# Log-sum-exp over rows: the first load from one contiguous block, its results stored early

## Chip, cores, metric

One core of one Trainium2 chip. The metric is the device time of one execution in microseconds (us); unless said otherwise a time is a median over runs of one kernel. All runs here were single-core, at a granted clock of 1.0. A profiled span is about 1.8 us shorter than the time of the same execution.

Loads are numbered as in the code, from 0 to 16. The prediction's "fifth load" is load 4.

## The reference

```python
# x: (32, 512, 1024) float32, drawn from N(0, 1); axis = -1
def reference(x, axis):
    x_max = np.max(x, axis=axis, keepdims=True)
    return (x_max.squeeze(axis) + np.log(np.sum(np.exp(x - x_max), axis=axis))).astype(np.float32)
```

There are 16384 rows of 1024 values (67.1 MB), and one result for each row. For this draw all results lie between 7.28 and 7.60. So the comparison with the reference cannot see results that are merely in the wrong place.

## The kernel before

Each of the 128 partitions owns 128 consecutive rows. They come in 17 loads of 1 to 16 rows a partition, all on SyncE's DMA queue, into a ring of 51 rows. ScalarE does Exp on each load. For the first `n_dve` rows of a load VectorE adds up the exponentials; for the others ScalarE adds them up itself, row by row. Two Ln instructions on ScalarE turn sums into results, and one store writes 64 KB at the end.

```python
CHUNKS = [   # rows a partition, rows summed by VectorE
    (4, 1), (15, 11), (16, 10), (16, 15), (16, 0), (14, 0), (12, 9), (9, 5), (7, 5), (5, 4),
    (4, 3), (3, 0), (2, 2), (2, 2), (1, 0), (1, 0), (1, 0),
]
RING_ROWS = 51
LN_AT = 5                     # the first Ln comes before load 5's work
...
    x_v = x_flat.rearrange("(p t) d -> p t d", p=P)                       # 512 KB from partition to partition
    out_v = bass.AP(tensor=out.tensor, offset=out.offset, ap=[[NB, P], [1, NB]])
...
    def load(i):              # waits until its ring rows are free, then
        ... nc.sync.dma_start(out=ring[:, s : s + r], in_=x_v[:, row : row + r]).then_inc(landed[i], 16)
...
    for i, (r, n_dve) in enumerate(CHUNKS):
        if i:
            load(i)
        if i == LN_AT:
            take_logs(0, logged, *done_before[i])
        nc.scalar.wait_ge(landed[i], 16)
        ... Exp, and the sums ...
    take_logs(logged, NB, dves, acts)
    nc.scalar.wait_ge(act_done, acts)
    nc.scalar.dma_start(out=out_v, in_=res).then_inc(stored, 16)
    nc.gpsimd.wait_ge(stored, 16)
```

The softmax here doesn't subtract the row's maximum and nothing guards it: scores larger than these inputs give would overflow.

## Time and profile before

| | before |
|---|---|
| time, 3 runs | 164.23 us (164.02 to 164.56) |
| span of the profiled run | 162.2 us |
| ScalarE busy | 124.1 us, 76% |
| load 0 / load 4 / load 5 has landed | 7.40 / 83.67 / 100.65 us |
| last wait of ScalarE for a load ends | 83.69 us |
| last store, issue to landing | 1.57 us |

The landing times and the store's 1.57 us are from the trace's records of semaphore updates, which have two digits; the page rounds them. A load has landed when the last of its 16 DMA queues has reported to its semaphore; on each queue it consists of eight packets. From the page of the kernel before (engines' busy time; DMA queues with packets, MB and the share of 16 DMA engines; issues with size and us to landing):

```profile
span 162.2 us, 213 instructions
DVE 72.9 (45%) x11; ACT 124.1 (76%) x136; POOL 0.2 (0%) x4
...
q1 hardware_dynamic: 2448, 67.11, 96.4%
q10 hardware_dynamic: 144, 0.07, 0.1%
q14 instruction: 1, 0.01, 0.0%
HBM read 67.11 MB, written 0.07 MB: 414 GB/s over the span
...
out_dram<-res ACTq DMA_DIRECT2D x1, 64.0 KB, 1.6
```

q1 carries all loads and is busy for 96.4% of the span, so DMA is the first limit. q14 is a fetch of instructions that the program does not ask for. The timeline of ScalarE (start, duration, line, operation; in brackets the idle time before it and what ended it) shows every wait for a load:

```profile
7.42 1.06 ACT L116 ACTIVATE ring<-ring 128x1024 f32<-128x1024 f32 x1 [5.37 <-DMA ring<-in_x_dram]
25.62 9.59 ACT L116 ACTIVATE ring<-ring 128x11264 f32<-128x11264 f32 x1 [14.02 <-DMA ring<-in_x_dram]
44.98 8.74 ACT L116 ACTIVATE ring<-ring 128x10240 f32<-128x10240 f32 x1 [5.62 <-DMA ring<-in_x_dram]
64.36 13.00 ACT L116 ACTIVATE ring<-ring 128x15360 f32<-128x15360 f32 x1 [4.42 <-DMA ring<-in_x_dram]
83.69 1.06 ACT L128 ACTIVATE ring<-ring 128x1024 f32<-128x1024 f32 x1 [5.29 <-DMA ring<-in_x_dram]
```

After 83.69 us ScalarE is busy without a break until the last store. But it is a close race: load 10 landed at 145.61 us and was used at 145.65, load 11 landed at 149.30 and was used at 149.34. Any delay of the stream over 0.04 us shows. Some pieces of the chain of waits (start, us, what), which has no load after 83.67 us:

```profile
47.15 36.52 DMA ring<-in_x_dram
83.67 0.02 issue
83.69 10.55 ACT ring L128 x21
...
148.40 4.16 ACT ring L128 x8
...
159.36 0.25 ACT res L93
```

Windows of the kernel before (stretch, its length, busy time of VectorE, ScalarE and GpSimd with the number of instructions, clock, DMA share, GB/s; a packet is counted whole where it starts, so short windows swing):

```profile
60.00:84.00 24.00, 11.17 (x2) 14.35 (x4) 0.00 (x0) 1.00 1.00 431
...
146.00:148.00 2.00, 2.00 (x1) 2.00 (x1) 0.00 (x0) 1.00 1.00 424
148.00:150.00 2.00, 2.00 (x2) 2.00 (x4) 0.00 (x0) 1.00 0.97 406
```

### The profile page before, as it was taken

The numbers are of one execution on the slowest core, as the hardware profiler recorded it, in microseconds if no ns is written. First come the engines' busy times: TensorE is split into PE (matmuls) and PEld (weight loads), VectorE is DVE, ScalarE is ACT, GpSimd is POOL, SyncE is SP. The second block draws the span as 40 slices with busy tenths as digits, with TensorE's granted clock in tenths as the row PEclk, the third lists the DMA queues.
The fourth block names the chain that finished last, engine by engine and source line by source line (L and its number), as shares of the span: only waits on it lengthen the run. The fifth ranks groups of instructions, "written<-read, shape, count | busy, mean of one in ns | idle before, by whom it ended". The sixth has DMA issues, their size and how long they took to land.

```text
span 162.2 us, 213 instructions
## 1 busy us (share of the span) xinstructions
DVE 72.9 (45%) x11; ACT 124.1 (76%) x136; POOL 0.2 (0%) x4
## 2 busy tenths in 40 slices
DVE  0030000039960799000999900000006999799591
ACT  3180006997099971999339999999999999999993
POOL 0000000000000000000000000000000000000000
DMA  6999899969969959969988999999999999999970
GB/s 263 497 485 470 349 394 517 485 291 517 485 291 517 517 259 517 517 275 501 517 368 370 424 424 432 461 497 388 436 427 399 431 400 439 420 424 414 415 318 16
DMA packets 2593, 67.18 MB, mean 414 GB/s; under 512 B 288, under 2 KB 416, under 8 KB 800
## 3 DMA queue, kind: packets, MB, share of 16 engines
q1 hardware_dynamic: 2448, 67.11, 96.4%
q10 hardware_dynamic: 144, 0.07, 0.1%
q14 instruction: 1, 0.01, 0.0%
HBM read 67.11 MB, written 0.07 MB: 414 GB/s over the span
## 4 chain that ended last, share of the span: by engine, by line
ACT 52%; DMA 38%; DVE 7%; issue 1%
DMA ring<-in_x_dram 38%; ACT ring L128 30%; ACT ring L116 22%; DVE sums L121 7%; ACT res L93 0%
## 5 line engine op out<-in xcount | busy, mean ns | idle before, releaser
L121 DVE TENSOR_REDUCE sums<-ring 128x5 f32<-128x5120 f32 (+8 forms) x11 | 72.9, 6648 | 86.0 <-ACT ring L116 85.9
L116 ACT ACTIVATE ring<-ring 128x5120 f32<-128x5120 f32 (+8 forms) x11 | 59.3, 5394 | 29.4 <-DMA ring<-in_x_dram 29.4
L128 ACT ACTIVATE ring<-ring 128x1024 f32<-128x1024 f32 x61 | 63.4, 1041 | 5.3 <-DMA ring<-in_x_dram 5.3
L128 ACT ACTIVATION_READ_ACCUMULATOR ring<-ring 128x1 f32 x61 | 11.4, 187 | 0.0
L103 ACT ACT_TABLE_LOAD x1 | 1.3, 1283 | 0.8 <-PEq L175 0.8
L93 ACT ACTIVATE res<-sums 128x67 f32<-128x67 f32 (+1 forms) x2 | 0.5, 256 | 0.1
L175 POOL MEMSET const-bfloat16-1.0<- 128x1 bf16 x1 | 0.1, 101 | 0.0
L175 POOL MEMSET const-uint8-127<- 128x1 uint8 x1 | 0.1, 101 | 0.0
L175 POOL MEMSET const-float32-0.0<- 128x1 f32 x1 | 0.1, 98 | 0.2 <-issue 0.2
L175 POOL MEMSET const-float32-1.0<- 128x1 f32 x1 | 0.1, 98 | 0.0
## 6 DMA issues: line engine op xcount, KB each, us to landing
ring<-in_x_dram SPq DMA_DIRECT2D x1, 7680.0 KB, 24.8
ring<-in_x_dram SPq DMA_DIRECT2D x1, 7168.0 KB, 36.1
ring<-in_x_dram SPq DMA_DIRECT2D x1, 6144.0 KB, 21.6
ring<-in_x_dram SPq DMA_DIRECT2D x1, 4608.0 KB, 32.1
ring<-in_x_dram SPq DMA_DIRECT2D x2, 2048.0 KB, 26.3
ring<-in_x_dram SPq DMA_DIRECT2D x1, 3584.0 KB, 40.2
ring<-in_x_dram SPq DMA_DIRECT2D x1, 2560.0 KB, 44.4
ring<-in_x_dram SPq DMA_DIRECT2D x2, 1024.0 KB, 46.0
```

What stands on the lines that cost most here:

```text
L93: nc.scalar.activation(out=res[:, lo:hi], in_=sums[:, lo:hi], func=Ln).then_inc(act_done, 1)
L103: nc.scalar.preload_act_table_set("natural_log_exp_and_others")
L116: nc.scalar.activation(out=ring[:, s : s + n_dve], in_=ring[:, s : s + n_dve], func=Exp).then_inc(act_done, 1)
L121: nc.vector.reduce_sum(out=sums[:, row : row + n_dve], in_=ring[:, s : s + n_dve], axis=AX).then_inc(dve_done, 1)
L128: nc.scalar.activation(out=ring[:, s + j], in_=ring[:, s + j], func=Exp, accum_out=sums[:, row + j : row + j + 1],).then_inc(act_done, 1)
L175: nc = _bacc.Bacc("TRN2", target_bir_lowering=False, num_devices=1)
```

## The change

The intent: the first load no longer picks 16 KB out of each 512 KB of the input but reads one contiguous 2 MB. Each partition's other 124 rows follow in the rest of the input, with 496 KB from partition to partition (the pitch). The results of the first four rows now belong elsewhere in the output than the other 124. So there are two stores: 128 pieces of 16 bytes, issued between loads 10 and 11 on the queue of the loads, and 128 pieces of 496 bytes at the end. Both are packed: the next partition's piece begins where this one's ends.

```diff
-FIRST_PARTS = [("sync", 0, 128)]
+STORE_AT = 11
...
-    x_v = x_flat.rearrange("(p t) d -> p t d", p=P)
-    out_v = bass.AP(tensor=out.tensor, offset=out.offset, ap=[[NB, P], [1, NB]])
+    R0 = CHUNKS[0][0]
+    x_first = x_flat[: P * R0].rearrange("(p t) d -> p t d", p=P)
+    x_rest = x_flat[P * R0 :].rearrange("(p t) d -> p t d", p=P)
+    out_first = bass.AP(tensor=out.tensor, offset=out.offset, ap=[[R0, P], [1, R0]])
+    out_rest = bass.AP(
+        tensor=out.tensor, offset=out.offset + P * R0, ap=[[NB - R0, P], [1, NB - R0]]
+    )
+
+    def rows_of(row, r):
+        return x_first if row == 0 else x_rest[:, row - R0 : row - R0 + r]
...
+        nc.sync.dma_start(out=ring[:, s : s + r], in_=rows_of(row, r)).then_inc(landed[i], 16)
...
+        if i == STORE_AT:
+            nc.sync.wait_ge(act_done, logs_done)
+            nc.sync.dma_start(out=out_first, in_=res[:, :R0]).then_inc(stored_first, 16)
         if i:
             load(i)
...
-    nc.scalar.dma_start(out=out_v, in_=res).then_inc(stored, 16)
+    nc.scalar.dma_start(out=out_rest, in_=res[:, R0:]).then_inc(stored, 16)
+    nc.gpsimd.wait_ge(stored_first, 16)
     nc.gpsimd.wait_ge(stored, 16)
```

More of the change, by code (lines that the diff above doesn't have):

```diff
@@ L54 @@
     dve_done = tc.alloc_semaphore("dve_done")
+    stored_first = tc.alloc_semaphore("stored_first")
     stored = tc.alloc_semaphore("stored")
@@ L83, in load @@
             nc.sync.wait_ge(act_done, act_wait)
-        for engine, lo, hi in FIRST_PARTS if i == 0 else [("sync", 0, P)]:
-            getattr(nc, engine).dma_start(
-                out=ring[lo:hi, s : s + r], in_=x_v[lo:hi, row : row + r]
-            ).then_inc(landed[i], 16)
+        nc.sync.dma_start(out=ring[:, s : s + r], in_=rows_of(row, r)).then_inc(landed[i], 16)
     def take_logs(lo, hi, dve_wait, act_wait):
@@ L113 @@
             take_logs(0, logged, *done_before[i])
-        nc.scalar.wait_ge(landed[i], 16 * (len(FIRST_PARTS) if i == 0 else 1))
+            logs_done = acts
+        nc.scalar.wait_ge(landed[i], 16)
         if n_dve:
```

## The prediction

> **What bounds the kernel now.** The DMA stream first, with ScalarE tuned to finish just behind it. The page gives 67.11 MB read at 414 GB/s; the windows view gives 431 GB/s from 60 to 84 us and 430 from 84 to 100 us. In the trace's packet records every engine's queue runs without gaps from about 1.1 to 157.6 us, and steady packets take 2.42 us for 65536 B, 2.27 us for 61440 B, 0.61 us for 16384 B: each is 27 GB/s per engine, 433 GB/s for 16. So steady packets already run at one common rate, whatever the address. ScalarE is busy 124.1 us (76%). In the chain of waits the fifth load lands at 83.67 us; from then ScalarE never waits again and ends at 159.6. The chunk landings in that tail are early by very little (chunks 10 and 11 by 0.04 us, the last by 0.11 us): DMA and ScalarE are level. Then the store: issue at 159.64, landing 1.6 us later.
>
> **What the change does.** Bytes read, chunk sizes and the order on ScalarE and VectorE stay. The row pitch between partitions goes from 512 KB to 496 KB, the first load becomes one contiguous 2 MB, SyncE gets one extra store (128 pieces of 16 B), the last store's pieces go from 512 to 496 B.
>
> 1. Start. The first packet of each engine is slow: by 0.00 to 0.75 us over the later 0.61 us, about 0.3 us in the mean; second packets are nearly clean. If this is the 512 KB pitch, up to 0.3 us are won, and the whole chain moves with it. If it is plain first latency, nothing is won. I count 0.15 us.
> 2. Pitch. The Trainium skill, "DMA: Bandwidth & Descriptors", section "Latency and other measured facts", warns of power-of-two HBM row pitches: 207 GB/s per direction at 512 KiB against 214 padded, for HBM-to-HBM copies. This trace shows no such loss after the first packets (under 0.2 us in all from 10 to 120 us): 0.0.
> 3. Early store. It sits between loads 10 and 11 in the same queue. The 512 B packets of the present store take 27 ns each, so an estimate of 0.1 to 0.2 us of queue time, just where ScalarE has 0.04 us of slack. SyncE's wait for the logs (done 100.7 us) is free, as load 11 is held to 103.9 us. Cost: 0.1 us.
> 4. Last store. 496 B pieces that start at odd multiples of 16 B; the same page gives 512 B as the size below which a read-modify-write happens. The landing might grow from 1.6 to 1.7 us: 0.05.
>
> All four are critical, and nearly cancel.
>
> **Predicted:** 164.1 us (range 163.5 to 164.7); faster by over 2%: 0.01, within 2%: 0.98, slower by over 2%: 0.01.
>
> **What would show it.** First-load landing at 7.1 to 7.4 us (before 7.40); fifth load within 0.4 us of 83.67; the windows view still 430 GB/s from 60 to 100 us; waits of ScalarE on loads 11 to 16 of 0 to 0.2 us; last store landing at 1.6 to 1.8 us; ScalarE still 124.1 us busy.
>
> **What would make it wrong.** The contiguous block could [...]slow the first load; the 16-byte writes could hold their queue by more than a microsecond, which the tail would feel in full; or unprofiled runs may suffer more from the start than the profiled one, so that the gain is larger than 0.3 us.

## The result, and the profile after

| | before | after |
|---|---|---|
| time, 6 runs each | 164.43 us (164.02 to 164.56) | 164.93 us (164.64 to 165.27) |
| ratio | | 1.0036, 95% interval 1.0019 to 1.0054 |
| profiled span | 162.2 us | 163.2 us |
| load 0 / 4 / 5 landed | 7.40 / 83.67 / 100.65 us | 7.75 / 83.93 / 101.18 us |
| load 11 landed | 149.30 us | 150.02 us |
| last store, issue to landing | 1.57 us | 1.76 us |

Every ratio in this document is the mean time of one kernel's runs over the mean of the runs of before in the same rounds, so not quite the ratio of the medians. The change makes the kernel slightly slower. Run again beside other kernels it came to 1.0015 (1.0000 to 1.0029). So it costs a quarter to six tenths of a microsecond, and the prediction's range (up to 164.7 us) did not hold the first measurement. Part of that is the base: the three runs of before had a median of 164.23 us, the six of the comparison 164.43 us.

The page of the changed kernel:

```profile
span 163.2 us, 215 instructions
DVE 72.9 (45%) x11; ACT 124.2 (76%) x136; POOL 0.2 (0%) x4
...
q1 hardware_dynamic: 2592, 67.11, 96.3%
q10 hardware_dynamic: 144, 0.06, 0.1%
q14 instruction: 1, 0.01, 0.0%
HBM read 67.11 MB, written 0.07 MB: 412 GB/s over the span
...
out_dram<-res ACTq DMA_DIRECT2D x1, 62.0 KB, 1.8
...
out_dram<-res SPq DMA_DIRECT2D x1, 2.0 KB, 45.4
```

The work of the engines is the same. q1 has 144 more packets, the early store: 128 pieces and 16 semaphore packets. It waits 45.4 us in the queue, which costs nothing as such. The waits for loads that the timeline of ScalarE marks, after:

```profile
7.77 1.06 ACT L128 ACTIVATE ring<-ring 128x1024 f32<-128x1024 f32 x1 [5.71 <-DMA ring<-in_x_dram]
25.88 9.59 ACT L128 ACTIVATE ring<-ring 128x11264 f32<-128x11264 f32 x1 [13.94 <-DMA ring<-in_x_dram]
45.25 8.74 ACT L128 ACTIVATE ring<-ring 128x10240 f32<-128x10240 f32 x1 [5.62 <-DMA ring<-in_x_dram]
64.61 13.00 ACT L128 ACTIVATE ring<-ring 128x15360 f32<-128x15360 f32 x1 [4.39 <-DMA ring<-in_x_dram]
83.95 1.06 ACT L140 ACTIVATE ring<-ring 128x1024 f32<-128x1024 f32 x1 [5.31 <-DMA ring<-in_x_dram]
101.20 1.06 ACT L140 ACTIVATE ring<-ring 128x1024 f32<-128x1024 f32 x1 [0.22 <-DMA ring<-in_x_dram]
```

Load 0 comes 0.35 us later, not earlier, and there is a new wait for load 5. The chain of waits now goes through loads 5 and 11 (the wait for load 11, 0.16 us, is not marked above):

```profile
64.87 36.31 DMA ring<-in_x_dram
101.18 0.02 issue
101.20 3.23 ACT ring L140 x6
104.44 0.02 issue
104.45 45.57 DMA ring<-in_x_dram
150.02 0.02 issue
150.05 3.23 ACT ring L140 x6
...
160.08 0.25 ACT res L101
```

And the windows show where the stream slowed, just behind the early store (its packets run at 144.5 to 145.7 us):

```profile
60.00:84.00 24.00, 11.20 (x2) 14.31 (x6) 0.00 (x0) 1.00 1.00 431
...
146.00:148.00 2.00, 2.00 (x1) 2.00 (x3) 0.00 (x0) 1.00 1.19 412
148.00:150.00 2.00, 2.00 (x2) 1.98 (x3) 0.00 (x0) 1.00 0.77 303
```

The added span of this pair of profiles, from the trace records, is 0.99 us:

- 0.53 us: load 5 lands later (0.26 us are there at load 4 already; 0.27 us come between loads 4 and 5);
- 0.19 us: from load 5's landing to the issue of the last store (58.99 us before, 59.18 us after), nearly all of it the wait for load 11;
- 0.19 us: the last store lands in 1.76 us, not 1.57;
- 0.08 us: the rest, after the store.

The timed runs differ by only 0.25 to 0.6 us, so single profiles scatter, and one pair must not be read too closely. The profile of before turned out to be the luckiest of the nine with that load layout (below).

### The profile page after: what moved, and what is told of

It is laid out like the page before. It is cut to its first block, busy times and chain, and to the rows that moved or that the text cites. A ratio compares the mean times of both kernels' runs of the same rounds, so it can differ in the third digit from the quotient of the medians.

```text
span 163.2 us, 215 instructions
## 1 busy us (share of the span) xinstructions
DVE 72.9 (45%) x11; ACT 124.2 (76%) x136; POOL 0.2 (0%) x4
## 4 chain that ended last, share of the span: by engine, by line
DMA 77%; ACT 13%; DVE 7%; issue 0%; SPq 0%
DMA ring<-in_x_dram 77%; ACT ring L128 8%; DVE sums L133 7%; ACT ring L140 6%; SPq L95 0%; ACT res L101 0%
```

## The experiments

Theory: three small costs, a slower start, an early store that holds up the loads behind it, and a slower last store. Rival 1: the layout of the loads does all of it. Rival 2: the stores do all of it, and the slow start was chance.

### E1 to E4: take the change apart

E1 drops the early store from the changed kernel (512 results are never written):

```diff
-        if i == STORE_AT:
-            nc.sync.wait_ge(act_done, logs_done)
-            nc.sync.dma_start(out=out_first, in_=res[:, :R0]).then_inc(stored_first, 16)
-    nc.gpsimd.wait_ge(stored_first, 16)
```

> The changed kernel without its early store and the wait for it; the 512 results of the first rows are never written, so the output is wrong on purpose. Theory (three small costs: slower first load about +0.25 us, early store about +0.2 us, 496-byte last store about +0.1 us): first load lands near 7.7 us, no wait of ScalarE on the tail loads, +0.3 us over before. Rival 1 (the address pattern of the loads alone): stays at +0.5 us. Rival 2 (the stores alone, the slow start of one profile was chance): +0.1 us and a first load at 7.4 us in the profile.

E2 also puts back the single store of before (results in the wrong place):

```diff
-    nc.scalar.dma_start(out=out_rest, in_=res[:, R0:]).then_inc(stored, 16)
+    nc.scalar.dma_start(out=out_v, in_=res).then_inc(stored, 16)
```

> The changed loads with the one 512-byte-a-partition store of before (results permuted, wrong on purpose). Theory: +0.25 us over before, first load near 7.7 us, last store lands 1.6 us after its issue. Rival 1: +0.5 us. Rival 2: 0.0 us.

E3 has the loads of before and both stores, with their pieces where before had those results (512 bytes from partition to partition):

```diff
+    out_first = bass.AP(tensor=out.tensor, offset=out.offset, ap=[[NB, P], [1, R0]])
+    out_rest = bass.AP(tensor=out.tensor, offset=out.offset + R0, ap=[[NB, P], [1, NB - R0]])
```

> The loads of before with the two stores of the change (16 bytes a partition early, 496 bytes at the end; output right). Theory: first load near 7.4 us, ScalarE waits up to 0.2 us on load 11, last store 1.75 us, +0.3 us over before. Rival 1: 0.0 us. Rival 2: +0.5 us.

E4 is E3 with the full 512-byte store at the end:

```diff
-    nc.scalar.dma_start(out=out_rest, in_=res[:, R0:]).then_inc(stored, 16)
+    nc.scalar.wait_ge(stored_first, 16)
+    nc.scalar.dma_start(out=out_v, in_=res).then_inc(stored, 16)
```

> The loads of before with the early 16-byte store, and at the end the full 512-byte store (it rewrites the early values; output right). Against the split-store run this takes away only the 496-byte pieces. Theory: +0.2 us over before, last store 1.6 us. If the 496-byte pieces cost nothing, it equals the split-store run; if the early store costs nothing, it equals before.

| | loads | early store | last store | ratio (95%) | load 0 / 5 landed, us | last store, us |
|---|---|---|---|---|---|---|
| E1 | changed | none | 496 B packed | 1.0015 (1.0002 to 1.0028) | 7.78 / 100.98 | 1.89 |
| E2 | changed | none | 512 B | 1.0007 (0.9995 to 1.0019) | 7.66 / 101.18 | 1.57 |
| E3 | before | 16 B, 512 apart | 496 B, 512 apart | 1.0014 (1.0001 to 1.0028) | 7.48 / 101.05 | 1.58 |
| E4 | before | 16 B, 512 apart | 512 B | 1.0006 (0.9994 to 1.0018) | 7.32 / 100.81 | 1.56 |

Neither rival gets the whole cost from one side: no part alone reaches 1.0036, but the intervals are as wide as the effects. The last store looked like the clear part. With packed pieces it took 1.89 us; with the same 496-byte pieces 512 bytes apart it took 1.58 us, so being under 512 bytes is not enough to slow it. So was the trouble with both stores their packing?

### E5: packed or apart

> The changed kernel once more, beside the three others of this call. Expected +0.3 to +0.6 us over before, first load near 7.7 us, last store near 1.8 us.

The next kernel is the changed one with both stores' pieces 512 bytes apart (results in the wrong place):

```diff
-    out_first = bass.AP(..., offset=out.offset, ap=[[R0, P], [1, R0]])
-    out_rest = bass.AP(..., offset=out.offset + P * R0, ap=[[NB - R0, P], [1, NB - R0]])
+    out_first = bass.AP(..., offset=out.offset, ap=[[NB, P], [1, R0]])
+    out_rest = bass.AP(..., offset=out.offset + R0, ap=[[NB, P], [1, NB - R0]])
```

> The changed kernel, with the same two stores written 512 bytes apart in the output, as before had it, where the change packs them densely (16 and 496 bytes apart); results permuted, wrong on purpose. Theory (the cost of both stores is that neighbouring pieces are packed without alignment, not that there are two stores or that they are small): at most +0.15 us over before, last store 1.6 us, no hold in the load queue at the early store. Rival (the small size and the extra DMA cost): equal to the changed kernel, +0.3 to +0.6 us.

Then E4 with the early pieces packed, and the kernel before with only the last store's pieces packed (512 results unwritten):

```diff
-    out_first = bass.AP(tensor=out.tensor, offset=out.offset, ap=[[NB, P], [1, R0]])
+    out_first = bass.AP(tensor=out.tensor, offset=out.offset, ap=[[R0, P], [1, R0]])
```

> The loads of before with the early store packed 16 bytes apart and at the end the full 512-byte store (which rewrites those bytes, output right). It differs from the run with the early store and the full store only by the spacing, 16 for 512 bytes. Theory: +0.2 to +0.3 us over before, ScalarE waits on load 11. Rival: +0.1 us, as that run.

```diff
-    out_v = bass.AP(tensor=out.tensor, offset=out.offset, ap=[[NB, P], [1, NB]])
+    out_v = bass.AP(tensor=out.tensor, offset=out.offset + P * 4, ap=[[NB - 4, P], [1, NB - 4]])
...
-    nc.scalar.dma_start(out=out_v, in_=res).then_inc(stored, 16)
+    nc.scalar.dma_start(out=out_v, in_=res[:, 4:]).then_inc(stored, 16)
```

> The loads of before, no early store, the last store in pieces of 496 bytes packed 496 bytes apart (the first 512 results stay unwritten, wrong on purpose). Theory: only the last store's landing grows, 1.57 to about 1.8 us, +0.2 us. Rival (the 496-byte store is free, its slower landing came by chance): 0.0 us and 1.6 us.

| | ratio (95%) | packets of load 11 over 0.5 us, of 128 | last store, us |
|---|---|---|---|
| changed kernel, first profile | 1.0036 (1.0019 to 1.0054) | 19 | 1.76 |
| changed kernel, again | 1.0015 (1.0000 to 1.0029) | 0 | 1.69 |
| both stores 512 apart | 1.0001 (0.9987 to 1.0014) | 0 | 1.57 |
| loads of before, early packed | 1.0014 (0.9999 to 1.0028) | 24 | 1.56 |
| loads of before, last packed | 1.0003 (0.9987 to 1.0019) | 0 | 1.61 |

A packet of load 11 (12288 bytes) takes 0.46 us when nothing holds it. In the two profiles with a hold, packets took up to 1.19 and 1.03 us. The store's own packets last 9 ns each, so their eight on each DMA queue account for 0.07 us only. It is the packets behind them that are slow. ScalarE felt it in the run with the early store packed (timeline of ScalarE):

```profile
150.03 1.06 ACT L141 ACTIVATE ring<-ring 128x1024 f32<-128x1024 f32 x1 [0.16 <-DMA ring<-in_x_dram]
```

With the pieces apart the changed kernel cost nothing measurable (1.0001). That fits packing as the cause, though its interval overlaps that of the changed kernel in the same call. But the repeat of the changed kernel had no hold at all, so a packed early store does not always do it. And the direct test of the last store missed: with only that store packed it landed in 1.61 us, not 1.8, and the time did not move (1.0003), as the rival had expected. Whether packing slows the last store stays open. To see the early store's effect without the scatter I made it eight times as large.

### E6: eight early stores, and the first load's address pattern

Eight early stores stand in a row, each with its own results, over which the full last store writes later. The packed and the spread kernel differ in one line:

```diff
-        bass.AP(tensor=out.tensor, offset=out.offset + P * R0 * k, ap=[[R0, P], [1, R0]])   # packed
+        bass.AP(tensor=out.tensor, offset=out.offset + R0 * k, ap=[[NB, P], [1, R0]])       # 512 bytes apart
```

> The loads of before, the full 512-byte store at the end, and eight early stores in a row of 16-byte pieces packed 16 bytes apart, each to its own 2 KB (rewritten at the end, output right). Theory (dense small pieces hold the load packets behind them in the same queues): the hold grows well beyond the 0.4 to 0.55 us an engine seen after one such store, ScalarE waits on load 11, at least +1 us over before. Rival (the cost is the number of small packets, 9 ns each): equal to the spread run, about +0.5 us.

> The same eight early stores with their 16-byte pieces 512 bytes apart. Theory and rival alike: 8 x 8 packets of 9 ns are 0.58 us of queue time an engine, so up to +0.5 us over before, and no load packet behind them over 0.5 us.

They cost the same: 1.0206 (1.0186 to 1.0227) packed and 1.0207 (1.0187 to 1.0228) apart, 3.4 us over before's 164.47 us. **My theory that spacing is what matters fell here.** Its rival fell too: 64 small packets on each queue at 9 ns are 0.58 us, not 3.4. First the windows of the packed one, then of the spread one, where the stream almost stops:

```profile
144.00:146.00 2.00, 1.90 (x2) 2.00 (x3) 0.00 (x0) 1.00 1.57 318
146.00:148.00 2.00, 2.00 (x1) 0.59 (x2) 0.00 (x0) 1.00 0.74 98
148.00:150.00 2.00, 1.47 (x1) 2.00 (x1) 0.00 (x0) 1.00 0.80 252
```

```profile
144.00:146.00 2.00, 1.90 (x2) 2.00 (x3) 0.00 (x0) 1.00 1.53 287
146.00:148.00 2.00, 2.00 (x1) 0.11 (x2) 0.00 (x0) 1.00 0.72 160
148.00:150.00 2.00, 1.53 (x1) 1.67 (x1) 0.00 (x0) 1.00 0.88 297
```

DMA moves 98 and 160 GB/s in the two microseconds after the stores, where 424 is normal, and ScalarE falls idle. Even load 10, which is ahead of the stores in the queue, landed late, at 147.44 and 148.30 us, where it is 145.6 to 146.0 in the five profiles of this layout with at most one early store. None of its packets took over 0.62 us, so only its reports to the semaphore came late; the trace does not show why. So two more runs asked for number and size. One has two spread stores (`range(2)`); the other has eight with pieces of 64 bytes:

```diff
-        bass.AP(tensor=out.tensor, offset=out.offset + R0 * k, ap=[[NB, P], [1, R0]])
+        bass.AP(tensor=out.tensor, offset=out.offset + 16 * k, ap=[[NB, P], [1, 16]])
...
-                nc.sync.dma_start(out=out_early[k], in_=res[:, R0 * k : R0 * k + R0]) ...
+                nc.sync.dma_start(out=out_early[k], in_=res[:, :16]) ...
```

> The loads of before, the full 512-byte store at the end and two early stores of 16-byte pieces 512 bytes apart (output right). If the cost is the number of small pieces, whatever their spacing (as the two runs with eight stores say): slow packets of load 11 and +0.2 to +0.5 us over before. If one spread store is free by its spacing: no slow packets, +0.1 us.

> As the eight spread early stores (+3.4 us), with pieces of 64 bytes that start on a multiple of 64 bytes in the output (values wrong until the full store rewrites them, so the output is right). If the size under a full line is what costs: slow packets behind the stores go away, under +1 us over before. If it is the number of pieces written to memory: +3 us again.

The "full line" of 64 bytes in the second expectation is a guess; no run here shows a line of that size. Two spread stores: 1.0015 (1.0002 to 1.0027), no slow packet of load 11. But load 10, ahead of them, landed 5.07 us after load 9, where it was 4.89 to 4.92 us in every profile with at most one early store, and ScalarE waited for it (it landed at 146.37 us and was used at 146.39). So in this profile spread stores were not free either. Eight with 64-byte pieces: 1.0049 (1.0033 to 1.0064), 0.8 us, a quarter of the 16-byte kind although they carry four times the bytes. Its windows:

```profile
144.00:146.00 2.00, 1.90 (x2) 2.00 (x3) 0.00 (x0) 1.00 1.16 348
146.00:148.00 2.00, 2.00 (x1) 2.00 (x3) 0.00 (x0) 1.00 1.01 363
148.00:150.00 2.00, 2.00 (x2) 1.93 (x3) 0.00 (x0) 1.00 0.96 408
```

So for a burst of stores the number of pieces is not what counts, since it is 1024 in all three runs. 16-byte pieces cost 0.42 us a store (3.4 us / 8), 64-byte pieces on 64-byte boundaries 0.10 us. Size and alignment changed together here, so these runs do not tell which of the two counts. In the burst of eight, spacing did not matter. With one or two stores slow packets showed only in packed ones (two profiles of three, against none of four spread, which are E3, E4, E5 and the two-store run). Whether spacing matters there, or three profiles simply caught it twice, stays open.

Two kernels of before changed only load addresses (wrong: some rows are read twice). In the first, load 0 alone is contiguous:

```diff
+    x_first = x_flat[: P * CHUNKS[0][0]].rearrange("(p t) d -> p t d", p=P)
...
-                out=ring[lo:hi, s : s + r], in_=x_v[lo:hi, row : row + r]
+            src = x_first if i == 0 else x_v[lo:hi, row : row + r]
```

> The kernel before with one thing changed: the first load reads one contiguous 2 MB; all other loads keep the 512 KB pitch, and the single store stays (a few rows are read twice, others never, so results are wrong on purpose). Theory (contiguity makes the first packets slow; the 496 KB pitch of the later loads gives it back): mean slowness of the first load's packets 800 to 950 ns an engine, first load at 7.6 to 7.8 us, fifth load at 84.0 to 84.4 us, +0.2 to +0.4 us over before. Rival (the pitch of the later loads has no effect): as the run with the changed loads and one store, +0.1 us, fifth load at 83.8 to 84.0 us.

In the second every load, load 0 too, steps 496 KB from partition to partition:

```diff
+    x_124 = x_flat[: P * 124].rearrange("(p t) d -> p t d", p=P)
+    x_124b = x_flat[P * 4 :].rearrange("(p t) d -> p t d", p=P)
...
+                in_=(x_124[lo:hi, :r] if i == 0 else x_124b[lo:hi, row - 4 : row - 4 + r])
```

> The kernel before with every load at a 496 KB pitch between partitions, the first one too (some rows read twice, wrong on purpose); single store. Theory: first load as before, 7.3 to 7.5 us with 400 to 700 ns of slowness an engine, and no slow packets later, fifth load at 83.6 us, -0.1 to -0.3 us against before. Rival: equal to before.

And two looks changed load 0's pitch alone, to 20 KB and 64 KB (`x_flat[: P * 5]` or `x_flat[: P * 16]` in place of `P * CHUNKS[0][0]`, of which each partition takes its first four rows):

> The kernel before with only the first load's pitch between partitions changed, from 512 KB to 20 KB (it reads from the first 2.5 MB of the input; values wrong on purpose). If it is contiguity that slows the first packets, about as before: 400 to 700 ns of slowness an engine. If it is the small stretch of memory, as the contiguous load: 800 to 1030 ns.

> The same with a pitch of 64 KB (the first 8 MB of the input). If the slowness falls as the stretch of memory grows: between the two, 500 to 900 ns. If contiguity alone matters: 400 to 700 ns.

Landing times from the trace records, as means where several profiles have the same loads:

| loads | profiles | load 0, us | load 1, us | load 4, us | load 5, us |
|---|---|---|---|---|---|
| as before (512 KB pitch) | 9 | 7.48 (7.32 to 7.61) | 25.78 | 83.95 | 100.98 |
| as changed (load 0 contiguous, rest 496 KB) | 6 | 7.73 (7.57 to 7.85) | 25.85 | 83.91 | 101.09 |
| load 0 contiguous, rest 512 KB | 1 | 7.66 | 25.81 | 83.86 | 100.90 |
| load 0 at 20 KB, rest 512 KB | 1 | 7.85 | 26.00 | 84.05 | 100.99 |
| load 0 at 64 KB, rest 512 KB | 1 | 7.21 | 25.30 | 83.36 | 100.60 |
| all at 496 KB | 1 | 7.32 | 25.46 | 83.51 | 100.70 |
| load 0 and most others at 448 KB (E7) | 1 | 7.26 | 25.38 | 83.43 | 100.96 |

The contiguous load 0 lands a quarter of a microsecond later on average. The calls ran on different chips, but in each call that had both kinds every contiguous load 0 landed after every one at a 512 KB pitch. But that is nearly gone at load 1, and at load 4 nothing is left: with the layout of before, slow packets go on into load 1. The kernel with load 0 alone contiguous took 0.9993 (0.9979 to 1.0007) of before, where my theory said +0.2 to +0.4 us. My idea that the contiguous start costs and the 496 KB pitch pays it back fell: load 1 is clean after a contiguous start at either pitch. The start costs about the same in both kernels by load 4, only spread differently.

The expectations name another figure, the slowness of load 0: what its packets took beyond the steady 0.61 us, summed for each queue, in the mean of the 16. It was 0.65 to 1.02 us in the seven profiles with a contiguous load 0 and 0.36 to 0.67 us in the nine of before. So contiguous addresses started slower, not faster. At 20 and 64 KB it was 0.48 and 0.49 us, as before: by what was written down, contiguity matters and not the small stretch of memory. The late landing at 20 KB is that of one queue (7.85 us, the next one 7.44). The slowness does not set the landing alone: at 448 KB it was 0.72 us, and load 0 landed early.

A start that is really faster is seen at 64, 448 and 496 KB for load 0, 0.3 to 0.5 us at load 1. Contiguity does not give it, and the look at 20 KB did not show it either. The trace does not show why, and each of these has one profile. All loads at 496 KB took 0.9979 (0.9964 to 0.9994), the only kernel here whose interval lies below 1.

### Where a faster start goes

The three kernels that were early at load 4 (83.36 to 83.51 us, 0.4 to 0.6 us ahead of the nine's mean) keep 0.0 to 0.4 us of that at load 5. Load 5 has 7.34 MB, 16.95 us at 27.06 GB/s on each of 16 queues. In most profiles all queues but one or two take just that, and one or two take 17.2 to 17.7 us. In every profile the instruction fetch of q14 (8 KB, 0.31 us, once 0.35, at 88.9 to 89.6 us) falls into that stretch, and it is the only other traffic there. In each of the 20 profiles the packet of load 5 that starts as the fetch ends took 2.36 to 2.50 us, where 2.12 is usual and no other took over 2.22. With the fetch itself that is 0.55 to 0.69 us on one queue. So I take the fetch for the cause, though no run removed it. A load counts as landed when its slowest queue is done. If the delayed queue was early, the fetch costs nothing; if all queues are level, it is added in full. From load 5 on things are rigid. In the kernel before, in E2, with load 0 alone contiguous, in the one with all loads at 496 KB and in the 20 KB look the span is load 5's landing plus 61.53 us (61.52 in the 64 KB look). What lies above that is late loads and slow stores.

### E7: the early store elsewhere, and a kernel meant to beat both

> The changed kernel with its early store issued after the last load instead of between loads 10 and 11; nothing else moves, output right. If the 16-byte store costs by holding the loads behind it: no slow packets of load 11, and the time of the run without the early store, +0.1 to +0.2 us over before. If the place in the queue does not matter: equal to the changed kernel, +0.2 to +0.6 us.

```diff
-        if i == STORE_AT:
-            nc.sync.wait_ge(act_done, logs_done)
-            nc.sync.dma_start(out=out_first, in_=res[:, :R0]).then_inc(stored_first, 16)
...
+    nc.sync.wait_ge(act_done, logs_done)
+    nc.sync.dma_start(out=out_first, in_=res[:, :R0]).then_inc(stored_first, 16)
     take_logs(logged, NB, dves, acts)
```

Result right, 1.0015 (1.0002 to 1.0027), no slow packets of load 11. That equals the run without the early store (1.0015), and the second measurement of the changed kernel too (1.0015), so it does not show a gain.

> A kernel meant to beat both, output right: the contiguous block is the third load (16 rows a partition, 8 MB), all other loads, the first too, have a pitch of 448 KB; both stores are made of pieces that are multiples of 64 bytes (64 bytes packed, after the last load; 448 bytes packed at the end). If the 512 KB pitch is what slows loads after the first (the run with every load at 496 KB was 0.21% faster): fifth load near 83.5 us, -0.2 to -0.4 us against before. If dense packing as such slows the last store: it lands in 1.7 us or more and takes 0.1 to 0.2 us of that back; if only pieces off a 64-byte line do, it lands in 1.6 us.

```diff
+BLOCK = 2                                   # the load that reads the contiguous block: 16 rows a partition
+    R0 = CHUNKS[BLOCK][0]                   # x_first, x_rest, out_first, out_rest as in the change
-    row = slot = 0
-    for r, _ in CHUNKS:
+    row, slot = R0, 0
+    for n, (r, _) in enumerate(CHUNKS):
-        place.append((slot, row))
+        place.append((slot, 0 if n == BLOCK else row))
-        row += r
+        row += 0 if n == BLOCK else r
```

Result right, 1.0005 (0.9993 to 1.0018). It was 0.5 us ahead at load 4 and had lost it at load 5, with the largest delay of all (17.52 us between the two landings):

```profile
83.45 1.06 ACT L137 ACTIVATE ring<-ring 128x1024 f32<-128x1024 f32 x1 [5.30 <-DMA ring<-in_x_dram]
100.98 1.06 ACT L137 ACTIVATE ring<-ring 128x1024 f32<-128x1024 f32 x1 [0.49 <-DMA ring<-in_x_dram]
```

Its last store, of 448-byte pieces packed on 64-byte boundaries, landed in 1.59 us (one profile). Packed 496-byte pieces, of whose common borders three in four lie off such boundaries, took 1.61 to 1.89 us in five profiles. As two of these took 1.61 us, this one profile does not settle whether the boundaries matter. No version was found that beats both kernels and has all its results in place.

## Why the prediction was wrong

- **What bounds the kernel**: right. DMA and ScalarE run level, steady windows are at 431 GB/s before and after, and every added delay of the tail showed.
- **Step 1, the start ("I count 0.15 us" of gain)**: wrong, this is the step that failed. Load 0 landed later, not earlier: by 0.25 us in the mean of the profiles (7.73 against 7.48), and at load 5 the changed loads stand 0.11 us behind (101.09 against 100.98), which is within the scatter of single profiles (100.65 to 101.22). What failed is the premise that slow first packets come from the 512 KB pitch and go away with contiguous addresses: load 0's slowness was 0.65 to 1.02 us a queue contiguous, against 0.36 to 0.67. No gain came of it: the changed loads with the old store took 1.0007 (0.9995 to 1.0019), load 0 alone contiguous 0.9993 (0.9979 to 1.0007). Why a contiguous load starts slower stays open. I had also taken one profile as the base, which at load 5 (100.65 us) was the earliest of nine.
- **Step 2, the pitch (0.0)**: right for steady packets. The Trainium skill, "DMA: Bandwidth & Descriptors", section "Latency and other measured facts", gives 207 GB/s per direction at a 512 KiB pitch in copies from HBM to HBM, and 214 for a 4 MiB pitch padded by 4 KiB. In these loads into SBUF windows of 431 GB/s were seen at both pitches.
- **Step 3, the early store (0.1 us, from 27 ns a packet)**: the size was near, the reason wrong. The packets took 9 ns. The cost is in the load packets behind them, up to 1.19 us in place of 0.46. It came to 0.19 us in the first profile and to almost nothing (0.05 us) in the second. Eight such stores cost 3.4 us where packet time gives 0.58 us.
- **Step 4, the last store (0.05 us)**: right in direction, its size open. Five profiles with packed 496-byte pieces landed in 1.61 to 1.89 us, 1.71 in the mean, against 1.57 us: 0.14 us. But the run that packed this store alone had 1.61 us and no measurable cost (1.0003). The size below 512 bytes, which I gave as the reason, was not it; 496 bytes at 512 apart took 1.58 us.
- **The sum**: 0.11, 0.1 (the mean of the two profiles) and 0.14 us are about 0.35 us slower, each of them no larger than the scatter of single profiles, and the two measurements give 1.0036 and 1.0015, or 0.6 and 0.25 us. My four terms add up to 0.0 us, and I had written 164.1, 0.1 us faster. A further 0.2 us of the miss came from the base of three runs, and a range of 0.6 us either way was too narrow for effects that single profiles could not settle.

## What to carry to other kernels

When a stream and an engine run level, count a change at the slowest of the DMA queues and at the last point where the engine waits, not where the change acts: here, of 0.4 to 0.6 us won at the start, between a third and all was gone within one more load. Don't cost small stores by their packets' own time; look at what runs behind them on the same queue, and keep pieces of a few bytes out of a queue that is critical. Before explaining a few tenths of a microsecond, get several profiles of the kernel before, as one may be the luckiest of nine.

## What the Trainium skill lacked or had wrong

- "DMA: Bandwidth & Descriptors" gives 512 bytes as the transfer size below which a read-modify-write takes place (section "Specifications"). Here size below 512 alone did no harm: 496-byte pieces 512 bytes apart landed in 1.58 us, as 512-byte pieces do (1.57), and 448-byte pieces packed on 64-byte boundaries in 1.59. Packed 496-byte pieces took 1.61 to 1.89 us. The landing times do not show whether a read-modify-write took place. The page does not say whether packed pieces with unaligned common borders land later, and these runs leave it open.
- The same page gives no cost for loads behind small stores on one queue (what it says of stalled writes is about DMA between cores): 1024 pieces of 16 bytes cost 3.4 us, the same number of 64-byte pieces on 64-byte boundaries 0.8 us, and with the 16-byte pieces DMA fell to 98 GB/s in a window of 2 us.
- No page tells what a first load's address pattern costs: load 0 (2 MB) landed at 7.57 to 7.85 us contiguous, at 7.32 to 7.61 at a 512 KB pitch and at 7.21 at 64 KB.
- "DMA: Bandwidth & Descriptors", section "Why a DMA increments its semaphore by 16 and not by 1", says that the up to 16 engines of a DMA finish independently, and the trace agrees: the 16 semaphore packets of load 0 run from 6.42 to 7.04 us. What it lacks is what one late queue can cost: in the kernel with a 448 KB pitch the last queue of load 5 reported at 100.96 us and the next at 100.38, and that undid a gain of all the others. That the instruction fetch of 0.31 us delayed this queue is inferred from its place in time.
